# Drawn priority offsets for sparse attention, and a memset for one clearing transfer, in a six-stage transformer kernel

## The chip, the cores and the metric

One Trainium2 chip, one core. The metric is the device time of the kernel in microseconds, the median of several runs. A core has TensorE (matmuls, with a queue of its own for loading weights), VectorE, ScalarE, GpSimd and SyncE; here SyncE issues all transfers. In the profile these are PE and PEld, DVE, ACT, POOL and SP.

## The reference

A sequence of 256 tokens of width 1024 goes through two layers of three parts each, and each part ends in a layer norm of `ALPHA * h + part(h)`:

```python
for layer in range(2):
    h = layer_norm(ALPHA * h + 0.5 * swiglu(h, ffn_w_in[layer, 0], ffn_w_out[layer, 0]), ...)
    mix = hybrid_mixer(h, ...) if layer == 0 else nsa_mixer(h, positions, ...)
    h = layer_norm(ALPHA * h + mix, ...)
    h = layer_norm(ALPHA * h + 0.5 * swiglu(h, ffn_w_in[layer, 1], ffn_w_out[layer, 1]), ...)
```

The hybrid mixer joins a gated delta rule (8 heads, chunks of 64 tokens) and a state-space scan. In the delta rule each chunk needs a solve with a unit lower triangular 64 x 64 matrix:

```python
a_low = where(strict, einsum('bhncd,bhnsd->bhncs', k_beta, k) * decay, 0.0)
sol = triangular_solve(a_low, rhs, left_side=True, lower=True, unit_diagonal=True)
```

The sparse attention (16 heads of 64 in two groups) is the gated sum of three attentions: over compressed blocks of keys (a small two-layer network makes them), over selected blocks, and over a window. With 256 tokens the selection takes every block, so the last two are plain causal attention with different keys and values.

## The kernel before

All six stages are one program: `('ffn', 'hyb', 'ffn', 'ffn', 'nsa', 'ffn')`, numbered 0 to 5; the sparse attention is number 4. Matmuls are done in two parts for precision: each weight tile is copied into a rounded half (`whi`, by ScalarE or VectorE) and a remainder (`wlo`, by VectorE), and each product takes three matmuls.

**The order of the work.** The Python code doesn't emit instructions at once. It records operations (`Plan.add`) with their dependencies and a priority, which is the operation's index in the recording (`op.prio = op.idx + self.base`). Where several strands of work shall run beside each other, `weave` records them in turns, by shares of TensorE time. In the hybrid mixer the strands are `delta`, `space`, `gate`, `space2` and `out_a`; in the sparse attention they are `attention`, `dense` (projections), `compressed` and `out_g0`. When all is recorded, `Plan.order` simulates the five engines with estimated durations and latencies: at every step it takes, on each engine, the ready operation that can start earliest, and among those that can start at once the one with the smallest priority. The order that results is emitted as it is; each engine then works through its own queue in that order and waits at whatever isn't ready. A change of one estimated duration or of one priority can thus change the order of other instructions too. The estimate for a transfer is its wait for the path, then its bytes by a rate, then some fixed time; for a gpsimd memset it is some fraction of a microsecond.

**The inverse (in `delta`).** The inverses of the 64 x 64 triangles are built from 16 x 16 ones in two levels (`lev` 4 and 5) for 16 blocks in each half of the partitions. Tiles: `X` holds the inverses, `Ys` (named Y) the transposed inverses of both token halves, `AT` the matrices and `Tt` (named T) the products between. T is 16 blocks of 64 columns. At level 4 `half(Tt, 0)` are the columns 0 to 15 and 32 to 47 of each block; at level 5 they are the columns 0 to 31. A level makes 64 matmuls `acc<-X,AT` into one bank, a VectorE multiplication from it into `half(Tt, 0)`, then 64 matmuls `acc<-Y,T` and 64 `acc<-T,Y`, and subtracts their results from Y and X. Those matmuls read all 64 columns of T, so the columns that a level doesn't write must be zero. T is cleared whole before level 4, and again between the levels:

```python
def zero(self, t):
    n = int(t.ids.size) // P
    ...
    self.nc.sync.dma_start(H3(t, n), self.zeros[:, None, :].to_broadcast([P, n, P]))
...
                if lev < 5:
                    self.zero(Tt)
```

The columns 32 to 47 are the ones that level 4 filled and level 5 doesn't write.

**The sparse attention.** Scores of four head pairs are made into a PSUM bank (`ps` or `acc`) by matmuls `ps<-fixed` (the causal mask) and `ps<-kd,qs`; VectorE takes the row maxima; ScalarE takes the exponentials, one instruction for each head, with the row sum (`P<-acc,arena`, `P<-ps,arena`); VectorE or ScalarE scale them; TensorE transposes them (`mp<-ident,P`), they are copied out (`PT<-mp`) and multiplied with the values (`acc<-PT,vtok`). Beside this `dense` makes the projections (`ps<-whi,x`, `ps<-wlo,x`), whose query part ScalarE copies out of its bank (`q<-ps`). The PSUM tags are `ps` (2 banks), `mp` (2) and `acc` (4), shared by the strands.

All instructions carry the same line, that of the emitting call, so the profile is read by tiles.

Of the kernel before, what the change touches and what calls it, by code (L numbers as in the profile page):

```python
# [40 lines left out]
NSA_SB = (("acc",), ("acc",), ("ps",), ("ps",))  # L41
CATCH = 1
ZERO_AT = 8

ENDS = 3

# [6 lines left out]
def H3(t, h):  # L53
    return t.rearrange("p (h t) -> p h t", h=h)
# [503 lines left out]
class K:  # L558
# [556 lines left out]
    def hybrid(self, x, then):  # L1115
        self.arena = None
        nc, i = self.nc, self.i
# [97 lines left out]
        for n, src in enumerate((kT, qT)):  # L1215
            sq = H3(self.m4(1024, "sq"), 4)
            nc.scalar.activation(sq, src, AF.Square)
            for h in range(4):
                o, c = n * 4 + h, h % 2
# [29 lines left out]
        def delta():  # L1249
# [40 lines left out]
            for j in range(15):  # L1290
# [3 lines left out]
                V.tensor_tensor(W[:, j + 1:, :j + 1], W[:, j + 1:, :j + 1], u, OP.subtract)  # L1294
                if j == ZERO_AT:
                    late = _Gate(self.plan, len(self.plan.ops) - 1)
# [5 lines left out]
            X, Tt = (H3(self.m4(1024, n, "D"), 16) for n in ("X", "T"))  # L1302
# [19 lines left out]
            for lev in (4, 5):  # L1322
                n = 1 << lev
                nb = 32 // n
                half = lambda t, q: t.rearrange("p h (j two i) -> p h j two i", two=2, i=n)[:, :, :, q, :]
                packed = lambda ps: ps.rearrange("p (h j i) -> p h j i", j=nb, i=n)
                m = lm[:, lev - 4, :].rearrange("p (j i) -> p j i", i=n)
                yield
                pT = self.bank("acc")
                for b, h, cp, k in heads:  # L1330
                    nc.tensor.matmul(pT[cp, k * 32:(k + 1) * 32], AT[b][cp, h, cp], half(X, 0)[cp, k], start=True, stop=True)
                V.tensor_tensor(half(Tt, 0), packed(pT), m[:, None].to_broadcast([P, 16, nb, n]), OP.mult)
                yield
                pX, pY = self.bank("acc"), self.bank("acc")
                for b, h, cp, k in heads:
                    nc.tensor.matmul(pY[cp, k * 32:(k + 1) * 32], Tt[cp, k, :], half(Ys[b][cp, :, cp], 1)[:, h],
                                     start=True, stop=True)
                for b, h, cp, k in heads:
                    nc.tensor.matmul(pX[cp, k * 32:(k + 1) * 32], Ys[b][cp, h, cp], half(Tt, 0)[cp, k], start=True, stop=True)
                for b, Y in enumerate(Ys):  # L1340
                    for cp in CP:
                        y = half(Y[cp, :, cp], 1)
                        V.tensor_tensor(y, y, packed(pY[cp, b * 256:(b + 1) * 256]), OP.subtract)
                V.tensor_tensor(half(X, 0), half(X, 0), packed(pX), OP.subtract)
                if lev < 5:
                    self.zero(Tt)

            yield
            pT = [self.bank("acc") for b in range(2)]
# [59 lines left out]
            for b, d in enumerate(blk):  # L1409
                tb = slice(b * P, (b + 1) * P)  # L1410
                attnT, vn = d['attnT'], d['vn']
                o = H3(self.m4(1024, f"o{b}"), 8)
# [138 lines left out]
        def out_a():  # L1551
# [3 lines left out]
            for s in range(4):  # L1555
                wo = self.unit_rows(w_out, 2 * s, 2, 0, D)
                for e in range(2):
                    for b in range(2):
                        for c in range(2):
                            cs = slice(c * 512, (c + 1) * 512)  # L1560
                            self.mm3(acc[b][c], self.xb(oT[0], b, 2 * s + e), (wo[e][0][:, cs], wo[e][1][:, cs]),
                                     s + e == 0, False)
                        yield
        self.weave(list(zip((delta(), space(), gate(), space2(), out_a()), W_HYB)))
        terms = []
        for s in range(4):
# [420 lines left out]
    def run(self, stages):  # L1987
        nc = self.nc
        self.ah = [None, None]
        self.first = True  # L1990
        x = self.new_x()

        warm = self.bank("acc")

        def spin(*heads):
            for n in heads:
                nc.tensor.matmul(warm[:, :n * P], self.ones, self.ones[:, None, :].to_broadcast([P, n, P]),
                                 start=True, stop=True)

        tab = self.one([P, 1], "tab")  # L2000
        nc.scalar.activation(tab, self.mhalf, AF.Silu)
        spin(4, 2)
        self.ah = [self.m4(D, f"h{b}", "L") for b in range(2)]

        def load(b, q):
            cs = slice(q * 512, (q + 1) * 512)
            nc.sync.dma_start(self.ah[b][:, cs], self.i['x'][0, b * P:(b + 1) * P, cs])
            self.transpose_half(x, b, self.ah[b], q)

        load(0, 0)  # L2010
        with _Gate(self.plan, len(self.plan.ops) - 3):
            spin(2, 2)
        self.arrivals = [[], [lambda: load(1, 0)], [], [lambda: load(0, 1), lambda: load(1, 1)]]
        for n, (kind, l, j, idx) in enumerate(stages):
            last = n == len(stages) - 1
            state = {}

            def then(b, acc, s, state=state, last=last, l=l, idx=idx):
                if b == 0:
                    state['x'] = None if last else self.new_x()  # L2020
                    state['gb'] = self.ln_params(l, idx)
                self.layer_norm(b, acc, s, state['gb'], state['x'], last)
            if kind == 'ffn':
                self.ffn(l, j, x, lambda b, acc: then(b, acc, 0.5), last)
            elif kind == 'hyb':
                self.hybrid(x, lambda b, acc: then(b, acc, 1.0))
            else:
                self.nsa(x, lambda b, acc: then(b, acc, 1.0))
            x = state['x']


STAGES = [('ffn', 0, 0, 0), ('hyb', 0, 0, 1), ('ffn', 0, 1, 2), ('ffn', 1, 0, 0), ('nsa', 1, 0, 1), ('ffn', 1, 1, 2)]
# [37 lines left out]
```

## Time and profile before

| | us |
|---|---|
| median of 3 runs | 1120.43 |
| lowest, highest | 1120.20, 1120.77 |
| profiled execution | 1120.57 |
| its span, first to last instruction | 1118.5 |

One execution was profiled, and the numbers of the profile are from it. Its stages by TensorE's work are, roughly: feed-forward 0 to 200 us, hybrid mixer 200 to 445, two feed-forwards 445 to 809, sparse attention 809 to 945, feed-forward to the end. A name like `ps<-whi,x` means: written tile, then the tiles read. In an order of instructions the columns are start, length, engine, operation, tiles, form and count, and in brackets the idle time of the engine ahead of it and what ended that. A list of waits has who waited for whom, the total, the number of times and the longest.

### The profile page before, as it was taken

What the parts mean: (1) busy time and instruction counts of PE and PEld (TensorE: products, weight loads), DVE (VectorE), ACT (ScalarE), POOL (GpSimd) and SP (SyncE); (2) the same over time, 40 slices, a digit from 0 to 9 for tenths busy, and PEclk for the clock granted to TensorE, in tenths of its full rate; (3) what the DMA queues carried; (4) which work ended last, traced back from release to release, by engine and by line L of the source; (5) the groups of instructions that cost most, each with busy time, mean ns of one, the idle gap of its engine ahead of it and who ended that gap; (6) DMA issues with size and microseconds to landing.
All of it is one profiled execution on the core that took longest, in us unless ns stands there. A gap on an engine that the chain in (4) does not pass through costs nothing.

```text
span 1118.5 us, 16483 instructions
## 1 busy us (share of the span) xinstructions
PE 1105.6 (99%) x6545; PEld 943.9 (84%) x6545; DVE 888.5 (79%) x1494; ACT 516.6 (46%) x930; POOL 56.3 (5%) x104
## 2 busy tenths in 40 slices
PE   9999999999999999999999999999999999999997
PEld 7888888899999788888888888888887678888886
DVE  6977768799979999777767977876879989777765
ACT  4635332278736545533423633433346776333320
POOL 1000000012001410000000000000000000000000
PEclk9999999999999999999999999999999999999999
DMA  9876562642933276755564665655426237755511
GB/s 335 302 252 199 183 219 80 188 133 55 271 114 105 85 241 211 263 188 188 189 192 146 236 213 184 201 182 164 150 71 232 76 113 248 242 188 195 181 39 38
DMA packets 148886, 198.37 MB, mean 177 GB/s; under 512 B 9389, under 2 KB 123722, under 8 KB 148810
## 3 DMA queue, kind: packets, MB, share of 16 engines
q1 hardware_dynamic: 148810, 197.33, 53.5%
q8 instruction: 51, 0.84, 0.3%
q14 instruction: 25, 0.20, 0.1%
HBM read 194.04 MB, written 1.05 MB: 174 GB/s over the span
## 4 chain that ended last, share of the span: by engine, by line
PE 87%; DVE 7%; ACT 2%; issue 2%; DMA 1%; POOL 1%; SPq 0%; DVEq 0%; ACTq 0%; POOLq 0%
PE ps L534 52%; PE acc L534 31%; PE mp L534 5%; DVE wlo L534 2%; DVE cv L534 1%; DVE arena L534 1%; DMA raw<-in_nsa_w_in_dram 1%; DVE o L534 0%; POOL arena L534 0%; DMA raw<-in_ffn_w_in_dram 0%; DVE AT L534 0%; ACT P L534 0%; DVE whi L534 0%; DVE y L534 0%; DVE qs L534 0%
## 5 line engine op out<-in xcount | busy, mean ns | idle before, releaser
L534 DVE TENSOR_TENSOR wlo<-raw,whi 128x1024 fp32r<-128x1024 f32 (+2 forms) x351 | 416.3, 1207 | 10.9 <-ACT whi L534 7.7
L534 PE MATMUL ps<-x,whi 128*128 128x512 f32 (+2 forms) x1584 | 369.1, 363 | 1.4 <-ACT cv L534 1.0
L534 PEld LDWEIGHTS ps<-x,whi 128*128 128x128 f32 (+1 forms) x1584 | 278.6, 188 | 46.1 <-ACT cv L534 2.9
L534 ACT ACTIVATE whi<-raw 128x1024 fp32r<-128x1024 f32 (+2 forms) x258 | 258.4, 1045 | 28.2 <-DMA raw<-in_ffn_w_in_dram 17.6
L534 PE MATMUL acc<-whi,g 128*128 128x512 f32 x698 | 228.4, 391 | 0.0
L534 PE MATMUL ps<-x,wlo 128*128 128x256 f32 x1368 | 222.4, 283 | 0.0
L534 ACT ACTIVATE sg<-ps 128x256 f32<-128x256 f32 x156 | 60.0, 385 | 343.4 <-PE ps L534 343.4
L534 PEld LDWEIGHTS ps<-x,wlo 128*128 128x128 f32 x1368 | 197.6, 190 | 11.3
L534 DVE TENSOR_TENSOR sg<-ps,sg 128x256 f32<-128x256 f32 (+1 forms) x158 | 67.4, 427 | 155.6 <-ACT sg L534 154.9
L534 PEld LDWEIGHTS acc<-whi,g 128*128 128x128 f32 x698 | 131.4, 188 | 25.8
L534 PE MATMUL acc<-wlo,g 128*128 128x512 f32 x349 | 136.9, 392 | 0.0
L534 PE MATMUL ps<-whi,x 128*128 128x512 f32 (+1 forms) x480 | 128.6, 385 | 0.0
L534 PEld LDWEIGHTS ps<-whi,x 128*128 128x128 f32 x480 | 85.7, 188 | 15.3 <-issue 0.8
L534 PEld LDWEIGHTS acc<-wlo,g 128*128 128x128 f32 x349 | 65.8, 189 | 10.8
L534 PE MATMUL acc<-whi,x 128*128 128x512 f32 x224 | 74.6, 405 | 0.3 <-DVE x L534 0.2
L534 PE MATMUL ps<-wlo,x 128*128 128x512 f32 (+1 forms) x240 | 67.2, 380 | 0.0
L534 DVE CAST whi<-raw 128x1024 fp32r<-128x1024 f32 (+2 forms) x93 | 63.4, 682 | 4.0 <-DMA raw<-in_nsa_w_in_dram 4.0
L534 PEld LDWEIGHTS acc<-whi,x 128*128 128x128 f32 x224 | 41.6, 188 | 10.3 <-DVE x L534 1.0
L534 PEld LDWEIGHTS ps<-wlo,x 128*128 128x128 f32 x240 | 43.3, 188 | 7.1
L534 POOL TENSOR_TENSOR lnve<-lnve,mhalf 128x1 f32<-128x1 f32 x12 | 11.5, 956 | 735.5 <-DVE lnve L534 735.5
L534 ACT ACTIVATE sg<-sg 128x256 f32<-128x256 f32 x72 | 30.2, 419 | 33.3 <-DVE sg L534 33.1
L534 PE MATMUL acc<-wlo,x 128*128 128x512 f32 x112 | 42.9, 398 | 0.0
(251 smaller groups left out, 1013.1 us busy)
## 6 DMA issues: line engine op xcount, KB each, us to landing
raw<-in_ffn_w_in_dram SPq DMA_DIRECT2D x72, 1024.0 KB, 5.1
raw<-in_ffn_w_out_dram SPq DMA_DIRECT2D x44, 1024.0 KB, 5.1
raw<-in_hyb_w_in_dram SPq DMA_DIRECT2D x20, 1024.0 KB, 5.3
raw<-in_ffn_w_in_dram SPq DMA_DIRECT2D x30, 512.0 KB, 4.9
raw<-in_hyb_w_out_dram SPq DMA_DIRECT2D x8, 1024.0 KB, 5.1
raw<-in_nsa_w_in_dram SPq DMA_DIRECT2D x5, 1024.0 KB, 5.6
raw<-in_nsa_cmp_w_dram SPq DMA_DIRECT2D x4, 1024.0 KB, 5.5
raw<-in_nsa_w_out_dram SPq DMA_DIRECT2D x4, 1024.0 KB, 6.1
```

The costliest lines, as they stand in the source:

```text
L534: r = getattr(getattr(nc, eng), fn)(*[res(a) for a in args], **{k: res(a) for k, a in kw.items()})
```

## The change

The clearing of T between the two levels is done by a gpsimd memset of the columns 32 to 47 of each block (`half(Tt, 0)[:, :, 1]` at level 4) in place of a transfer of zeros over the whole tile. And after all stages are recorded, the priorities of stage 4 get offsets: each run of 8 consecutive operations one number from a standard normal distribution (seed 180 x 10 + 4), times 3.0. The table `ORDER` names stage 4 alone; stage 1, the hybrid mixer, has no entry.

```diff
+ORDER = {
+    4: [(180, 3.0, 8)],
+}
...
                 V.tensor_tensor(half(X, 0), half(X, 0), packed(pX), OP.subtract)
                 if lev < 5:
-                    self.zero(Tt)
+
+                    nc.gpsimd.memset(half(Tt, 0)[:, :, 1], 0.0)
...
+        self.marks = []
         for n, (kind, l, j, idx) in enumerate(stages):
+            self.marks.append(len(self.plan.ops))
...
+        ends = self.marks[1:] + [len(self.plan.ops)]
+        for n, terms in ORDER.items():
+            a, e = self.marks[n], ends[n]
+            for number, spread, run in terms:
+                off = np.random.default_rng(number * 10 + n).standard_normal((e - a) // run + 2)
+                for o in range(a, e):
+                    self.plan.ops[o].prio += spread * off[(o - a) // run]
```

## The prediction

> **What bounds the kernel now.** I read the page's first two parts, then the busy times by stage, then the waits of TensorE's two queues, and last the orders of instructions around the two edits.
>
> The page first: each engine's busy time, share of the span and instructions.
>
> ```profile
> span 1118.5 us, 16483 instructions
> PE 1105.6 (99%) x6545; PEld 943.9 (84%) x6545; DVE 888.5 (79%) x1494; ACT 516.6 (46%) x930; POOL 56.3 (5%) x104
> ```
>
> TensorE is the bound: of 1118.5 us only 12.9 (1118.5 - 1105.6) are without a matmul. The number of matmuls is the same before and after, so the change can only move the time by way of TensorE's gaps. The stretches that the two edits can reach are the rest of the hybrid mixer from the clearing on (312 to 445 us) and the sparse attention (809 to 945), here with its tightest 20 us. Columns: the stretch, its length, the busy time of each engine, then the granted clock, the DMA engines' share and GB/s.
>
> ```profile
> 312.00:445.00 133.00, 132.55 (x980) 114.88 (x977) 120.94 (x198) 68.09 (x101) 25.59 (x40) 1.00 0.44 147
> 809.00:945.00 136.00, 133.75 (x838) 103.88 (x837) 117.63 (x228) 90.16 (x247) 8.65 (x24) 1.00 0.42 142
> 860.00:880.00 20.00, 18.18 (x118) 13.64 (x117) 19.66 (x43) 19.23 (x66) 2.65 (x5) 1.00 0.23 68
> ```
>
> The clock is 1.00 in all three. TensorE idles 0.45 us (133.00 - 132.55) in the hybrid's rest, and 2.25 us (136.00 - 133.75) in the attention. Of that, 1.82 lie between 860 and 880, where VectorE (19.66 of 20) and ScalarE (19.23 of 20) are both full. There, and only there, TensorE is not alone the bound: what it needs comes from two engines without slack, and their order decides how long it waits. The waits of the matmul queue in 809 to 945, and under them those of the weight-load queue (total, times, longest); the load queue runs ahead, so its waits show pressure that a matmul still in the array partly hides.
>
> ```profile
> PE ps L534 <- ACT q L534: 1.3, 1, 1.3
> PE mp L534 <- ACT P L534: 0.5, 1, 0.5
> PE mp L534 <- DVE q L534: 0.4, 1, 0.4
> ...
> PEld ps L534 <- ACT q L534: 1.5, 1, 1.5
> PEld mp L534 <- ACT P L534: 1.0, 3, 0.7
> PEld acc L534 <- ACT P L534: 0.9, 4, 0.3
> PEld mp L534 <- ACT arena L534: 0.5, 2, 0.3
> PEld ps L534 <- ACT P L534: 0.5, 2, 0.3
> PEld mp L534 <- DVE kd L534: 0.4, 1, 0.4
> PEld mp L534 <- ACT whi L534: 0.4, 1, 0.4
> PEld mp L534 <- DVE PT L534: 0.4, 1, 0.4
> PEld acc L534 <- ACT x L534: 0.2, 1, 0.2
> PEld mp L534 <- DVE hr L534: 0.2, 1, 0.2
> PEld acc L534 <- DVE kd L534: 0.2, 1, 0.2
> ```
>
> Two sums are used below. The matmul queue waited 1.3 + 0.5 + 0.4 = 2.2 us for another engine. The load queue waited 1.5 + 1.0 + 0.9 + 0.5 + 0.5 + 0.4 + 0.4 + 0.4 + 0.2 + 0.2 + 0.2 = 6.2 us, nearly all for ScalarE: the softmax (P) and the copy of the query projection (q) out of its bank.
>
> **Edit 1, the clearing of T.** Removed is one transfer of zeros issued from SyncE's queue between the two levels of the inverse. Added is one gpsimd memset of the 16 columns of each of 16 blocks (256 elements in a partition) that level 5's own write of T doesn't cover. What happens around it, in order of time, and last how long the transfer took to land:
>
> ```profile
> 259.75 0.61 POOL L534 TENSOR_SCALAR_AFFINE_SELECT sw<-sw 128x256 f32<-128x256 f32 x1 [2.25 <-DMA sw<-zeros]
> 312.67 0.60 SPq L534 DMA_DIRECT2D T<-zeros  x1
> 313.49 0.69 DVE L534 TENSOR_TENSOR X<-X,acc 128x512 f32<-128x512 f32 x1
> 314.62 2.06 PE L534 MATMUL acc<-X,AT 64*64 64x32 f32 x64
> 316.76 0.69 DVE L534 TENSOR_TENSOR T<-acc,arena 128x512 f32<-128x512 f32 x1 [2.58 <-PE acc L534]
> 331.43 1.34 POOL L534 TENSOR_SCALAR_AFFINE_SELECT bm<-arena 128x512 fp32r<-128x512 f32 x2 [71.07 <-PE acc L534]
> 319.89 0.37 SPq L534 DMA_DIRECT2D raw<-in_hyb_w_out_dram  x1
> L534 POOL MEMSET zeros<- x1: 204/204/204, 0.9 to 0.9; 128x128 f32 x1
> DMA to landing us min/median/max: 4.0/4.0/4.0
> ```
>
> The transfer lands at 312.67 + 4.0 = 316.67. The write of T at level 5 also needs the 64 matmuls into its bank, and these end at 314.62 + 2.06 = 316.68. Both arrive together, so with the transfer gone the write still starts at 316.76 at the earliest 0.08 us sooner: the direct gain is 0 to 0.08, and I take 0, because the releaser the row names is TensorE. The memset's own length: 204 ns for 128 elements gives 0.2 as a lower bound, twice that 0.41 by elements, and the 256-element select's 0.61 is the upper one. Its start is when level 4's matmuls have read T, about 312.6 (where the transfer was issued), so it ends by 313.3, 3.4 us ahead of the matmuls that read T next (after 316.76 + 0.69). GpSimd has nothing between 260.36 (259.75 + 0.61) and 331.43, so nothing queues behind it; if it were placed behind that select instead, 15 us late, the inverse would wait, but an order by readiness has no cause to do that. On SyncE's queue the next transfer leaves at 319.89, 6.6 us after the removed one (312.67 + 0.60): it waits for a free buffer, not for the queue, and does not come sooner. The removed 512 KB of traffic frees a path that is busy 0.44 of this stretch. So edit 1 is worth 0 by itself.
>
> It has a second way to act. The order of every instruction is computed ahead by a planner that estimates when each operand is ready. A zeroing that costs microseconds there and now costs a fraction of one moves the planned times, and any order from 312 us on may come out otherwise. What that can be worth is bounded by the waits of the load queue on other engines in 312 to 445:
>
> ```profile
> PEld mp L534 <- DVE x L534: 0.8, 1, 0.8
> PEld ps L534 <- ACT cv L534: 0.2, 1, 0.2
> PEld mp L534 <- POOL bm L534: 0.2, 1, 0.2
> ```
>
> That is 1.2 us at best. I give the same 1.2 to the other side, an estimate, since a shuffled order is as likely to make such a wait as to remove one. Value 0, ends -1.2 and +1.2. The feed-forward stages that follow do not see it.
>
> **Edit 2, the offsets.** Each run of 8 consecutive operations of the attention stage gets one drawn number, times 3.0, added to its priority, which otherwise is its index. Two neighbouring runs differ by 3.0 x 1.41 = 4.2 positions on the average draw. No instruction is added or removed. What changes is which of several ready operations goes first on an engine, and also when weight transfers are issued, with the same offsets. Operations of the weave's four strands stand side by side in index, so a shift of four positions is enough to put a PSUM evacuation ahead of a softmax operation, or behind it. The case in point, ScalarE's order (the first two, and the copy), the matmul that needed it, and a later block of eight softmax rows by its first and last:
>
> ```profile
> 870.63 0.49 ACT L534 ACTIVATE P<-acc,arena 128x256 f32<-128x256 f32 x1
> 871.08 0.62 ACT L534 ACTIVATE PT<-mp 128x512 f32<-128x512 f32 x1
> 872.00 0.64 ACT L534 ACTIVATE q<-ps 128x512 f32<-128x512 f32 x1
> 872.69 0.50 PE L534 MATMUL ps<-fixed 128*128 128x512 f32 x1 [1.31 <-ACT q L534]
> 875.27 0.35 ACT L534 ACTIVATE P<-ps,arena 128x128 f32<-128x128 f32 x1
> 878.14 0.41 ACT L534 ACTIVATE P<-ps,arena 128x128 f32<-128x128 f32 x1
> ```
>
> The q copy stands behind softmax work, and the bank it empties is the one the next scores are written to. Two places earlier (before 870.63) it would start 1.37 us (872.00 - 870.63) sooner, and the whole wait of 1.31 is gone. By such swaps the offsets can win at most what TensorE waits for others, 6.2 us by the load queue; the bound on the other side is in the rivals. I take 2.2, the three waits that the matmul queue itself shows, plus 0.9, the short waits on softmax into acc banks, which the same ScalarE order makes: 3.1, half the ceiling. Not more, because with 19.66 and 19.23 of 20 us busy the two engines only pass the waits on between 860 and 880. What is late next is VectorE there, whose 0.34 us of slack in those 20 hold nothing more.
>
> **Sum.** The profiled execution took 1120.57 us: its span of 1118.5 and 2.07 around it, 0.14 above the median of 1120.43. 1120.57 + 0 - 3.1 = 1117.47; against the median 1120.43 - 3.1 = 1117.3.
>
> **The rivals.** *Waits only change places.* For it: a number drawn without looking at ready times has no direction. Against: waits are bunched in one short piece, so a draw has more to undo than to do elsewhere, where TensorE's queue is never dry. It gives 1120.4, within 1.2 either way by the first edit; that the offsets alter nothing at all (ready times, not priorities, decide) gives the same.
>
> *Slower: a block of softmax moves ahead of an evacuation.* The block of eight above takes 878.14 + 0.41 - 875.27 = 3.28 us on ScalarE. If the draw puts one such block ahead of a bank's copy between 860 and 880, TensorE stands still for it: 1120.43 + 3.28 = 1123.7. It decides as soon as the block stands before a copy that TensorE already waits for, since ScalarE has only 0.77 us of those 20 to make it good. For it: the copy is already the longest wait, and offsets push as readily as they pull. Against: TensorE has dense projections ready to fill in during most of the stage, and idles 0.43 us outside those 20 us.
> A dearer form is a further pair of table switches, as the softmax's exponential and the other functions alternate:
>
> ```profile
> 856.42 0.60 ACT L534 ACTIVATE q<-ps 128x512 f32<-128x512 f32 x1 [4.85 <-PE ps L534]
> 857.04 1.28 ACT L534 ACT_TABLE_LOAD   x1
> 858.33 0.48 ACT L534 ACTIVATE P<-acc,arena 128x256 f32<-128x256 f32 x1
> ```
>
> Copy, load and next function follow without a gap, so a switch is 1.28 us and a pair 2.56: 1123.0 by itself, inside the range. The Trainium skill, "ScalarE: Activation LUTs", section "What ACT_TABLE_LOAD costs", adds a drain of about 1380 ns to a load of about 1283, 2.66 us a switch; by that a pair would give 1125.8. The trace agrees with the load and shows no drain after or before this one (856.42 + 0.60 = 857.02).
>
> **How the numbers follow.** About 0.2% (2.24 us) is what a measurement of this kernel can tell from no change. The forecast, 1117.3, has 0.50: with 3.1 us it clears that by 0.9. Its own range is 1113.0 to 1118.2 (all 6.2 and the 1.2; down to 2.2 alone). Waits that change places have 0.19, the slower block 0.28, the switch pair 0.03. So faster 0.50, same 0.19, slower 0.31. The range for 8 in 10 reaches from 1120.43 - 6.2 - 1.2 = 1113.0 to 1123.71 + 1.2 = 1124.9; outside lie a wait dearer than one block, and a gain that the load queue doesn't show.
>
> **What would show it.** Right: in the attention, TensorE's idle time falls from 2.25 us towards none, the 1.3 us wait on ScalarE's q copy is gone, the stage is about 3 us shorter; the hybrid from 200 to 445 and all feed-forward stages keep their lengths within 1.2; the memset stands alone on GpSimd near 313 us, and T's write is still released by TensorE. Wrong: a longer wait of TensorE on ScalarE or VectorE between 860 and 880, a further table load in the stage, or a difference of over 1.2 us that arises before 445 us, which would make the clearing and not the offsets the cause.

## The result, and the profile after

The changed kernel takes 1118.08 us (median of 19 runs, 1117.45 to 1119.0), the kernel before 1120.51 beside it (19 runs, 1120.2 to 1121.1): ratio 0.9979, 95% interval 0.9973 to 0.9985, so 2.4 us faster. The profiled execution of after took 1118.67 us, 0.59 above its median.

The page of after, for comparison with the one of before: span, then busy time of each engine.

```profile
span 1116.8 us, 16492 instructions
PE 1103.7 (99%) x6545; PEld 944.8 (85%) x6545; DVE 886.6 (79%) x1494; ACT 516.6 (46%) x932; POOL 56.2 (5%) x103
```

The same 6545 matmuls are busy for 1.9 us less (1105.6 - 1103.7); outside them lie 13.1 us where there were 12.9. The whole gain is in TensorE's busy time and none of it in its idle time. The prediction took each operation's engine as fixed, but the planner may give some operations to one of several engines: in the attention GpSimd now does two fewer (`q<-arena`, 4 for 6), and ScalarE does two more. The windows say the same of the stages (columns as before):

```profile
312.00:445.00 133.00, 132.56 (x968) 114.84 (x965) 120.99 (x198) 68.12 (x101) 25.95 (x41) 1.00 0.42 143
808.66:943.10 134.44, 132.01 (x839) 104.39 (x837) 117.16 (x229) 89.98 (x250) 8.12 (x22) 1.00 0.43 147
860.00:880.00 20.00, 18.92 (x128) 14.74 (x127) 19.78 (x48) 18.20 (x59) 2.82 (x6) 1.00 0.24 75
```

The hybrid mixer's rest is as it was. The second row is the stretch that answers to 809 to 945 of before: busy 132.01 against 133.75, idle 2.43 against 2.25. Between 860 and 880 TensorE idles less (1.08 for 1.82), and it idles more elsewhere. To measure a stage without choosing borders, I take the last matmul of the feed-forward ahead of the attention and the first `acc<-whi,g` behind it, from the timelines of before and of after:

```profile
800.34 0.39 PE L534 MATMUL acc<-whi,g 128*128 128x512 f32 x1
955.99 0.40 PE L534 MATMUL acc<-whi,g 128*128 128x512 f32 x1
```

```profile
800.00 0.39 PE L538 MATMUL acc<-whi,g 128*128 128x512 f32 x1
954.08 0.40 PE L538 MATMUL acc<-whi,g 128*128 128x512 f32 x1
```

This stretch, called the attention's length below, was 155.65 us and is 154.08: 1.57 of the 1.90 us between the two profiled executions. The other 0.34 is there at 800 us already; it arises in the first 21 us, where the order is the same, and differs from run to run (the feed-forward's last matmul starts between 799.94 and 800.76 us in all kernels below that leave the hybrid mixer's order alone).

**The clearing.** The tile T in the timeline of after:

```profile
312.38 0.31 POOL L538 MEMSET T<- 128x256 f32 x1 [52.40 <-PE acc L538]
316.37 0.69 DVE L538 TENSOR_TENSOR T<-acc,arena 128x512 f32<-128x512 f32 x1 [2.55 <-PE acc L538]
```

The memset is done at 312.69 us, and the write of T still starts when TensorE's matmuls release it.

**The waits.** TensorE's matmul queue in the attention of after:

```profile
PE mp L538 <- DVE arena L538: 1.0, 1, 1.0
PE ps L538 <- ACT q L538: 0.7, 1, 0.7
PE mp L538 <- DVE qT L538: 0.4, 1, 0.4
PE acc L538 <- ACT x L538: 0.3, 1, 0.3
```

The wait on the q copy has halved (0.7 for 1.3), those on P and on VectorE's q are gone, and three others came, the longest at 845 us, ahead of all softmax: 2.4 us in all, 2.2 before. What fell is in the load queue, in the lines named "issue", where the profile shows nothing that it waits for. First before (809 to 945), then after (808 to 944):

```profile
PEld mp L534 <- issue: 8.0, 21, 0.8
PEld acc L534 <- issue: 2.5, 9, 0.4
PEld ps L534 <- issue: 1.8, 3, 0.8
```

```profile
PEld mp L538 <- issue: 6.9, 22, 0.8
PEld acc L538 <- issue: 2.7, 9, 0.4
PEld ps L538 <- issue: 0.8, 1, 0.8
```

12.3 us became 10.4. That is about what the matmuls' busy time lost, and it fits a smoother order of the same matmuls; what an "issue" consists of the profile does not show, nor that the two are one thing.

**What was reordered.** The first visible difference that shifts other engines is at 832 us. TensorE, then SyncE's queue, before and after:

```profile
832.14 1.06 PE L534 MATMUL mp<-raw,X 128*32 128x256 f32 x12
833.13 1.08 PE L534 MATMUL acc<-PT,vtok 128*64 128x512 f32 x4
834.14 1.49 PE L534 MATMUL mp<-raw,X 128*32 128x256 f32 x20
834.80 1.23 SPq L534 DMA_DIRECT2D raw<-in_nsa_w_in_dram  x2
```

```profile
831.80 1.07 PE L538 MATMUL mp<-raw,X 128*32 128x256 f32 x16
832.80 1.08 PE L538 MATMUL acc<-PT,vtok 128*64 128x512 f32 x4
833.82 1.07 PE L538 MATMUL mp<-raw,X 128*32 128x256 f32 x16
832.94 2.38 SPq L538 DMA_DIRECT2D raw<-in_nsa_w_in_dram  x2
```

`mp<-raw,X` are the compression network's matmuls, 32 records for 16 matmuls and two weight tiles. Before, the first tile's eight were cut into six and two around the value matmuls, so its `raw` buffer came free a microsecond late. After, the eight are together, and the next weight transfer into that buffer leaves 1.86 us earlier (0.34 of that was there at 800 us already). The shift is seen further on: ScalarE's first use of that tile, VectorE's remainder of the keys, and after only, the first exponential, two copies of the queries (before had the first exponential at 858.33, the copies at 856.42 and 872.00):

```profile
840.16 1.06 ACT L534 ACTIVATE whi<-raw 128x1024 fp32r<-128x1024 f32 x1 [7.55 <-DMA raw<-in_nsa_w_in_dram]
853.08 0.69 DVE L534 TENSOR_TENSOR kd<-mp,kd 128x512 fp32r<-128x512 f32 x1
```

```profile
838.22 1.06 ACT L538 ACTIVATE whi<-raw 128x1024 fp32r<-128x1024 f32 x1 [5.71 <-DMA raw<-in_nsa_w_in_dram]
851.06 0.69 DVE L538 TENSOR_TENSOR kd<-mp,kd 128x512 fp32r<-128x512 f32 x1
854.84 0.47 ACT L538 ACTIVATE P<-acc,arena 128x256 f32<-128x256 f32 x1 [2.96 <-DVE arena L538]
858.36 0.60 ACT L538 ACTIVATE q<-ps 128x512 f32<-128x512 f32 x1
870.64 0.60 ACT L538 ACTIVATE q<-ps 128x512 f32<-128x512 f32 x1
```

The softmax starts 3.49 us earlier, in time in which ScalarE stood idle before (its 4.85 us ahead of 856.42). The copy at 858.36 now stands behind five exponentials instead of ahead of them, and no matmul waits for it. The last copy comes 1.36 us earlier.

### The profile page after: what moved, and what is told of

The parts are those of the page before. It is cut to its first block, busy times and chain, and to the rows that moved or that the text cites. A ratio compares the mean times of both kernels' runs of the same rounds, so it can differ in the third digit from the quotient of the medians.

```text
span 1116.8 us, 16492 instructions
## 1 busy us (share of the span) xinstructions
PE 1103.7 (99%) x6545; PEld 944.8 (85%) x6545; DVE 886.6 (79%) x1494; ACT 516.6 (46%) x932; POOL 56.2 (5%) x103
## 4 chain that ended last, share of the span: by engine, by line
PE 87%; DVE 8%; ACT 2%; issue 2%; DMA 1%; POOL 1%; DVEq 0%; ACTq 0%; POOLq 0%
PE ps L538 52%; PE acc L538 31%; PE mp L538 4%; DVE wlo L538 2%; DVE arena L538 1%; DVE cv L538 1%; DMA raw<-in_nsa_w_in_dram 1%; ACT whi L538 1%; DVE o L538 0%; POOL arena L538 0%; DVE whi L538 0%; DVE AT L538 0%; DVE y L538 0%; DVE x L538 0%; DVE h L538 0%
```

## The experiments

Each time is a median, beside before in the same session. The table gathers them; "estimate" is what the kernel's own planner makes of the order, less its value for before. It is no measurement, and is shown for what it is worth.

| kernel | us | before | ratio, 95% interval | attention's length | estimate |
|---|---|---|---|---|---|
| before | | | | 155.65 | 0 |
| after | 1118.08 | 1120.51 | 0.9979 [0.9973, 0.9985] | 154.08 | -1.26 |
| memset_only | 1120.67 | 1120.45 | 1.0002 [0.9993, 1.0011] | 155.57 | 0 |
| offsets_only | 1117.66 | 1120.45 | 0.9976 [0.9967, 0.9986] | 153.57 | -1.26 |
| draw_224 | 1118.35 | 1120.45 | 0.9981 [0.9973, 0.9990] | 153.96 | -1.15 |
| draw_181 | 1122.58 | 1120.45 | 1.0019 [1.0010, 1.0028] | 157.75 | +4.29 |
| draw_0 | 1121.49 | 1120.52 | 1.0009 [1.0000, 1.0018] | 156.81 | +1.97 |
| runs_35_52_53_76 | 1117.93 | 1120.38 | 0.9977 [0.9968, 0.9986] | 153.17 | -1.26 |
| runs_35_52_53 | 1120.75 | 1120.52 | 1.0005 [0.9996, 1.0014] | 156.16 | +1.60 |
| run_35 | 1121.43 | 1120.38 | 1.0011 [1.0003, 1.0020] | 157.28 | +2.22 |
| whole_tile | 1118.97 | 1120.38 | 0.9992 [0.9983, 1.0001] | 154.14 | +0.57 |
| hybrid_148 | 1119.29 | 1120.38 | 0.9990 [0.9981, 0.9999] | 153.19 | -2.19 |
| whole_22 | 1119.85 | 1120.52 | 0.9990 [0.9981, 0.9999] | 153.35 | -1.34 |
| whole_22_again, one run | 1119.76 | 1120.55 | | 154.61 | -1.34 |

**Each half alone.** memset_only empties the table of offsets, offsets_only keeps the transfer:

```diff
 ORDER = {
-    4: [(180, 3.0, 8)],
 }
```

```diff
-                    nc.gpsimd.memset(half(Tt, 0)[:, :, 1], 0.0)
+                    self.zero(Tt)
```

> The memset in place of the transfer, and no offsets. If the clearing is worth nothing (my account: the transfer and the matmuls it stood beside ended at the same time, and the planner's estimated span comes out the same to the nanosecond with either), it takes 1120.5 us, within 0.3 of the kernel before. If the clearing carries the gain (rival), it takes about 1118.1.

> The offsets alone, T cleared by the transfer as before. If the offsets carry the whole gain (my account) it takes 1118.1 us, within 0.4 of the changed kernel. If the clearing carries it (rival), 1120.5.

The clearing does nothing, within 0.1%: its order of instructions is that of before on every engine, but for the one instruction. The offsets are the whole gain: alone they give 2.79 us, the change 2.43, and the two intervals overlap.

**Other draws.** The same line with another number in place of 180.

```diff
-    4: [(180, 3.0, 8)],
+    4: [(224, 3.0, 8)],
```

> The changed kernel with another draw: number 224 in place of 180, same spread and run length. Its planned span (the planner's own estimate) is 1.15 us under that of no offsets, that of 180 is 1.25 under. If the estimate ranks orders as the chip does, it takes about 1118.3 us. If a draw has no direction that the estimate knows of, anything from 1117 to 1123; if any offsets help by loosening the order, 1118.

> The changed kernel with number 181 in place of 180. Its planned span is 4.29 us over that of no offsets. If the estimate ranks orders as the chip does, it takes 1122 to 1125 us, the slower rival of the prediction. If any offsets help by loosening the order, 1118; if draws do nothing but change places of waits, 1120.5 within 1.

> The memset, and offsets of another draw, number 0, taken because it is the first and not for any result. By the kernel's own estimate it is 1.97 us above before, near the middle of 240 draws. Theory A: a draw has no direction, and the draw of the change is one that was on the good side: 1120 to 1122.5, with a wait on q or P of over 1.5 us between 860 and 880. Theory B: what helps is any disorder that breaks the weave's turns, as the three draws that made the first compression tile whole might suggest: 1117.5 to 1119.

Number 224, picked for its low estimate, is about as fast as the change; 181, picked for its high one, is 2.13 us slower than before, and 0, picked for nothing, 0.97 slower. So a draw has no direction, and number 180 lies on the good side; the estimate puts 168 of the draws 0 to 239 above before, 24 level with it and 48 below, and 180 lowest of all. (Draw 0 is not quite in the middle: 82 of the 240 lie above it.) In 181 TensorE stands still once for the copy of the queries; ScalarE, then TensorE, in the timeline of draw_181:

```profile
872.02 0.65 ACT L538 ACTIVATE q<-ps 128x512 f32<-128x512 f32 x1
872.73 0.50 PE L538 MATMUL ps<-fixed 128*128 128x512 f32 x1 [2.72 <-ACT q L538]
```

Lined up by its matmuls and counted from the stage's start, it had been about 1.6 us ahead of before at 867 us and was level with it at 884; it lost 2.1 us at 924 to 928, where the attention hands over to the feed-forward and matmuls waited for the layer norm (0.7 us for `h`, 0.3 for `x`). draw_0 loses 2.1 us at the same place, where it had been 1.0 ahead; its wait on the q copy is 1.4 us, just under the 1.5 expected, and did not put it behind. TensorE at the handover, first in draw_181, then in draw_0:

```profile
927.01 1.29 PE L538 MATMUL mp<-ident,h 128*128 128x128 f32 x8 [0.66 <-DVE h L538]
```

```profile
928.43 3.70 PE L538 MATMUL ps<-whi,x 128*128 128x512 f32 x15 [0.92 <-DVE x L538]
```

**Which of the offsets.** The stage has 166 runs of 8 operations. Offsets for four of them (35, 52, 53 and 76) alone, then for 35 alone, then for 35, 52 and 53:

```diff
                 for o in range(a, e):
-                    self.plan.ops[o].prio += spread * off[(o - a) // run]
+                    if (o - a) // run in (35, 52, 53, 76):
+                        self.plan.ops[o].prio += spread * off[(o - a) // run]
```

> The changed kernel with 4 of its 166 drawn offsets kept (runs 35, 52, 53 and 76 of stage 4) and the others at zero. Its planned span equals that of all offsets, 1.25 us under none. If these four carry the gain (my account now: a few exchanges, of which the rest are bystanders) it takes 1118 us within 0.6; if the gain is spread over many small exchanges (rival), about 1120.3.

> One offset alone, run 35 (softmax scalings and transposes just ahead of the compression's matmuls). Its planned span is 2.22 us over that of none. If the planner's estimate holds, 1121.5 to 1122.7. If the earlier release of the first compression tile (which it brings about) is by itself the cause of the gain (rival), about 1118.5.

> The offsets of runs 35, 52 and 53 alone; it differs from the kernel with the four runs (1117.93 us) only in that run 76 (the first copy of the queries out of their bank, two exponentials and their transposes) keeps its old priority. Theory A: the gain needs two things, the compression weight tile whole, so that the next weight transfer goes out about 1.5 us earlier, and an order of the softmax after 855 us in which the last copy q<-ps isn't pushed behind a row of exponentials. Without run 76 the second is lost: the transfer raw<-in_nsa_w_in still goes out near 833.5, but TensorE waits over 2 us for q, and the time is 1120.4 to 1121.8, like run 35 alone (1121.43); the kernel's own estimate is 1.6 us above before. Theory B: the early transfer carries the gain and run 76 is worth nothing: 1117.9 +- 0.6, and no wait on q over 1.3 us.

Four offsets of 166 carry all of it. Run 35 alone makes the tile whole (its transfer leaves at 833.52) and is slower all the same, by a 2.73 us wait for the q copy at 872.10, behind six exponentials in a row, and by a stretch of halved clock behind that wait (last section). With 52 and 53 beside it that wait is 0.4, so the first theory was right on the time of runs_35_52_53 and wrong on its place. Lined up by its matmuls, this kernel is 1.8 us ahead of before at 912 us (0.4 at 800) and no longer ahead at 930. It loses that at the last block of the attention; TensorE in its timeline:

```profile
913.86 1.09 PE L538 MATMUL mp<-ident,P 128*128 128x128 f32 x8 [0.78 <-ACT PT L538]
915.61 1.08 PE L538 MATMUL mp<-PT,vtok 128*64 128x512 f32 x4 [0.66 <-DVE PT L538]
```

The last exponentials came at 909.58, the projection's matmuls were used up, and the copies out of the transposes had nothing to hide behind. With run 76, which holds two early exponentials, the first copy of the queries and their transposes, the value matmuls follow at 912.90 without a wait. A gain made at 832 us can thus be given back at later places, and run 76 alone changes nothing in the planner's order.

**The whole tile by hand.** No draw; the first tile's eight compression matmuls get a priority ten places ahead:

```diff
+                        if v == 0 and h == 0:
+                            self.plan.ops[-1].prio -= 10
```

> No draw at all: the eight matmuls on the first compression weight tile get priority 10 places earlier, so that they are no longer split 6 + 2 by the value matmuls, the tile's buffer is free about 1.9 us sooner and the next weight transfer leaves as much sooner. Everything behind follows the planner; planned span 0.57 us over that of none. If the earlier transfer by itself carries the gain, 1118 to 1119; if it has to come with the right order behind it, as the estimate says, 1120.4 to 1121.5.

Its PE and SyncE rows:

```profile
831.19 1.93 PE L538 MATMUL mp<-raw,X 128*32 128x256 f32 x32
832.32 1.23 SPq L538 DMA_DIRECT2D raw<-in_nsa_w_in_dram  x2
```

The attention is 1.51 us shorter and the median 1.41 lower, though the estimate said 0.57 longer. This is the gain's first part, made without any draw. The edit moves the transfer (2.48 us earlier) and also puts all 32 records in one piece; the two were not tried apart. The interval reaches to 1.0001, because three of its eleven runs are at 1120.3 to 1122.1; those three have a mean granted clock of 0.995 to 0.997, the other eight 0.998 or 0.999 (see the last experiment).

**Where the time is won and lost.** To line a kernel up with before, the matmuls done since the stage's start are counted, each kind at its mean length over these runs; a lead found so is an estimate, good to some 0.3 us. At 860 us whole_tile is 1.7 us ahead of before, run_35 and draw_181 are 1.4, the kernel with the four offsets is 1.2, and after is only 0.3, since it has paid its 1.0 us wait at 845. Between 860 and 880 after and the four offsets gain another 1.1 us; their waits there are 0.7 and 0.4, where before has 1.3 and 0.5. In the same 20 us whole_tile loses 0.3, draw_181 1.4 and run_35 3.5. So the gain has two parts: one before 860, which every kernel here with the early transfer shows, and one at the copy of the queries, which hangs on the order there.

**Looking for a better order.** A draw for the hybrid mixer beside the change's own, and a draw of spread 6.0 on top of the whole tile, both the lowest of their kind by the estimate:

```diff
 ORDER = {
+    1: [(148, 6.0, 8)],
     4: [(180, 3.0, 8)],
 }
```

```diff
-    4: [(180, 3.0, 8)],
+    4: [(22, 6.0, 8)],
...
+                        if v == 0 and h == 0:
+                            self.plan.ops[-1].prio -= 10
```

> The changed kernel with offsets in the hybrid mixer as well (number 148, spread 6.0, runs of 8), chosen by its planned span, 0.93 us under the changed kernel's. If the estimate ranks orders of that stage as the chip does, about 1117.2 us; if the hybrid mixer's waits are too few for any order to win, 1118.1 within 0.5; above 1119 if the estimate misleads there.

> The memset, the first compression weight tile's eight matmuls moved up by ten places by hand, and on top of that offsets of draw 22 with spread 6.0, the lowest of 476 by the kernel's own estimate with that edit (1.34 us below before, 0.09 below the change's own). Theory A (the estimate sorts orders within the attention, to about 1.5 us): 1116.5 to 1118.5, a transfer raw<-in_nsa_w_in before 833.5 and no wait on q over 1.3. Theory B (the estimate is no guide at this size, as for the orders with a hybrid draw and with the whole tile alone): anywhere from 1117 to 1121.

Neither beats the change. The hybrid draw costs more than it was to gain: the last matmul ahead of the attention starts at 801.95 us, 1.61 later than before (0.17 of that is there after 20 us, ahead of the mixer). The whole tile with draw 22 has two groups of times, five runs of 1118.1 to 1118.6 us at a mean granted clock of 0.998 and six of 1119.9 to 1120.3 at 0.996 to 0.997. The first theory's signs came (the transfer at 832.97 us, no wait on q), its time only in the quick group. One more profile of the same kernel took 1119.76 us at 0.996, beside the second group:

> The kernel with the whole tile by hand and draw 22 once more, for one further profile: its eleven times fall into two groups, five of 1118.1 to 1118.6 us at a mean granted clock of 0.998, and six of 1119.9 to 1120.3 at 0.996 to 0.997. The first profile is of the quick group and shows the clock at 1.00 until 1110 us. Theory A (TensorE's granted clock is halved for some us after an idle piece of the attention, as in the profile of run 35 alone between 872 and 879 us): a profile at about 1120 shows a stretch of about 4 to 8 us at 0.5 in the attention and the loss of about 1.8 us right there. Theory B (the difference lies in transfers or at the start): a profile at about 1120 has the clock at 1.00 throughout the attention. A profile at about 1118.3 tells nothing.

Two windows of whole_22, then the two of whole_22_again that hold the same work, 0.25 us earlier on its clock (the column after POOL is the granted clock):

```profile
871.20:874.61 3.41, 2.62 (x19) 1.85 (x17) 3.41 (x10) 2.33 (x9) 1.24 (x4) 1.00 0.00 0
874.61:878.03 3.42, 3.30 (x17) 1.98 (x17) 3.34 (x7) 3.38 (x13) 0.00 (x0) 1.00 0.14 29
```

```profile
870.95:874.36 3.41, 2.62 (x19) 1.86 (x17) 3.41 (x10) 2.32 (x9) 1.25 (x4) 1.00 0.00 0
874.36:877.78 3.42, 3.34 (x9) 2.54 (x10) 3.34 (x7) 3.34 (x12) 0.00 (x0) 0.50 0.08 16
```

The instructions and the gaps between them are the same up to 874 us; then one run has the clock at 0.50 for 3.42 us, does 9 matmuls where the other does 17, and is behind for good: its attention is 1.26 us longer. Theory A was right on the place and the kind, and too high on both sizes (4 to 8 us, a loss of about 1.8). So the second group is the granted clock, as far as one profile and the mean clocks of eleven runs show it, and the kernel's quick group (median 1118.16) is no faster than the change.

## Why the prediction was right, and where not

- **TensorE is the bound, and only its gaps can move.** Half right. The stage was right, and no other engine became the bound. But the time came out of "busy": 133.75 to 132.01 us for the same matmuls. Busy time as recorded holds delays between matmuls too, and the prediction took it as fixed.
- **The clearing, 0, with ends of 0 and 0.08.** Right: memset_only 1.0002, the write of T still released by TensorE, and the memset 0.31 us, between the predicted 0.2 and 0.61.
- **The planner's new order in the hybrid, 0 within 1.2.** Right, and it was exactly 0: the planner's order stays the same.
- **The offsets, 3.1 us.** The sign and about the size were right: 2.43 measured, 2.79 alone; 1.57 in the two profiled executions, where after has one wait of 1.0 us on `arena` that is 0.5 in offsets_only. The step behind it failed. It was 2.2 us of matmul-queue waits and 0.9 of the load queue's waits for P; the former are 2.4 us after, and the idle time that should have gone towards none is 2.43. That 3.1 came near the 2.4 is therefore luck in good part. The ceiling of 6.2 was read too kindly as well: 3.9 of it were waits for P and q, 5.0 for ScalarE at all. (And 4.2 positions is the standard deviation of the difference between two neighbouring runs; its mean size is 3.4.)
- **The mechanism named for it, the q copy two places ahead of the softmax.** Wrong in the way, and right in a part of the place. The last copy did come earlier (872.00 to 870.64) and its wait fell from 1.3 to 0.7, but because all that stands before it began earlier: in both orders 76 instructions of ScalarE that write P stand ahead of it in the stage, and the copy before that moved the other way. (It also took more than two places to get ahead of 870.63: an exponential at 871.55, not among the rows shown, stands there too.) Of the 1.1 us gained between 860 and 880, 0.7 is idle time that is gone. The other part of the gain is made before 860, and there the prediction left a term at nothing: it said that offsets also change when weight transfers are issued, and put no price on it. whole_tile shows 1.4 to 1.5 us for the order with the whole tile and the early transfer; in the profiled execution of after a new wait of 1.0 us at 845 takes most of that part back.
- **Waits only change places.** In sum that is what TensorE's waits did (2.2 us before, 2.4 after); the time fell beside them, in the busy time.
- **Slower: a block of softmax ahead of an evacuation.** It did not happen in this draw, but the mechanism is real: 2.72 us in draw_181 and 2.73 in run_35, for 3.28 predicted. The price was about right for the wait, and left out that such a wait can be paid again in the clock. In draw_181 the wait only used up a lead of about 1.4 us. The place where draw_181, draw_0 and runs_35_52_53 fall behind, the end of the attention (912 to 930 us), was not seen: TensorE had no wait there in before.
- **A further pair of table switches.** There was none: 21 loads before and after.
- **The chances.** The one unpicked draw is slower than before, and by the estimate seven in ten are; by that, 0.50 for faster was high and 0.31 for slower low, whatever number 180 then did.

## What to carry to other kernels

Where one engine is full, look at what frees the buffers of its weight transfers: eight matmuls cut in two around others held a buffer for a microsecond, and keeping them together, which also sent the next transfer off sooner, was worth about 1.4 us here. Priorities only break ties of readiness, so of many offsets a few act, and an early gain must survive the places downstream where the cover is thin; measure an order as a whole, since a planner's estimate here had the sign wrong once in eleven and sizes off by up to 2.2 us. Then read the granted clock: a short idle piece on TensorE may cost its length again.

## What the runs showed of the hardware

The granted clock of TensorE fell to half within the kernel, after a stretch in which TensorE still worked for a part of the time. (In every profile it also falls to half at the very end, after 1111 us.) The matmul that ended the wait in run_35's timeline, then two windows of run_35 around it:

```profile
872.80 0.79 PE L538 MATMUL ps<-fixed 128*128 128x512 f32 x1 [2.73 <-ACT q L538]
```

```profile
869.07:872.48 3.41, 1.01 (x7) 0.74 (x5) 3.41 (x7) 3.41 (x14) 0.00 (x0) 1.00 0.38 87
872.48:879.30 6.82, 6.34 (x22) 4.61 (x24) 6.52 (x16) 5.64 (x23) 1.71 (x4) 0.50 0.35 114
```

For 6.82 us the clock is 0.50. What that costs is an estimate: 3.42 us at 0.50 made the attention of whole_22_again 1.26 us longer, so 6.82 us would cost about 2.5. Lined up by its matmuls, run_35 falls back by 3.5 us between 860 and 880, and 1.4 of that is its longer wait (2.73 for 1.31), which leaves about 2.1. All eleven runs of run_35 have a mean clock of 0.995 to 0.997, where before and after have 0.998 to 0.999 in every run: its loss is the wait and the clock together, and where it would stand against before at full clock is not known.

In whole_22_again the stretch is 3.42 us, half of 6.82, which looks like a fixed window. The clock's own records bear that out: the stretches at full clock last 1109.33 us in before, 1105.92 in after, 1112.75 in draw_181, and 866.99 and 238.93 in run_35, which are 325, 324, 326, 254 and 70 times 3.4133. The Trainium skill, "TensorE: Matmul & The Clock Gate", section "What's actually happening", gives a free-running window of 3413 ns, which the traces agree with, and says that the clock halves after at least one idle window. That differs from what is seen here: the 3.41 us ahead of the halving had 1.01 us of matmuls in run_35 and 2.62 in whole_22_again, whose longest gap was 0.37 us.

Why it halves in some runs and not in others hangs in part on where the windows fall. draw_181's profile has the same 2.72 us wait at full clock. Counted back in steps of 3.4133 us from where its clock falls at the end, its windows cut that wait in two, where run_35's window above held most of it:

```profile
868.38:871.79 3.41, 1.63 (x12) 1.30 (x9) 3.41 (x8) 3.41 (x14) 0.00 (x0) 1.00 0.01 2
871.79:875.20 3.41, 2.41 (x15) 1.94 (x15) 3.41 (x10) 3.41 (x15) 0.76 (x1) 1.00 0.48 155
```

What is counted in a window stays open. It is not the busy time: 1.63 us kept the clock in draw_181, 2.62 did not in whole_22_again. The columns that a window's matmuls write (the 512 of a form 128x512) fit better: 1792 and 1536 in the windows ahead of the two halvings, at most 2304 ahead of those at the end, and no fewer than 2304 in any other window of the 14 profiles. That count was found by trying several on the same traces, and no run tests it. Nor does a lower mean clock always cost time: seven of draw_181's eleven runs have 0.996 or 0.997 and take 1122.35 to 1123.29 us, the other four, at 0.998, 1122.30 to 1122.72.
